# Both parts of every third weight unit made by GpSimd DMAs in a decoder layer with weights split in two

## The chip, the cores and the metric

The kernel runs on one core of a Trainium2 chip as a single program. A core has TensorE (matmuls; its weight loads are shown apart), VectorE, ScalarE, GpSimd and SyncE, each with its own queue of instructions that it works off in order, and 16 DMA engines that all queues share. The metric is the device time of one execution in microseconds, lower is better. The median of three runs before the change is 1499.94 us (1499.26 to 1501.11).

## The reference

One layer of a hybrid decoder on 256 tokens of width 2048, in float32. A normalised input goes through one large projection; its columns feed two mixers side by side (a gated DeltaNet with 8 heads and a block-sparse attention with 8 heads), both mixers are projected back, gated and added, and a gated feed-forward of inner width 5632 follows. Cut to what matters:

```python
u = _rmsnorm(h, norm_mix_w[l])
proj = jnp.einsum('btd,de->bte', u, w_in[l])
(q_a, k_a, v_a, z_a, beta_a, dec_a, q_b, k_b, v_b, gate_a, gate_b) = jnp.split(proj, split_at, axis=-1)
y_a = _gated_deltanet(q_a, k_a, v_a, z_a, beta_a, dec_a, conv_w[l], a_log[l], dt_bias[l], gdn_o_norm_w[l])
y_b = _moba_attention(q_b, k_b, v_b, q_norm_w[l], k_norm_w[l], rel_bias)
mix = (jax.nn.sigmoid(gate_a) * jnp.einsum('btc,cd->btd', y_a, w_branch_gdn[l])
       + jax.nn.sigmoid(gate_b) * jnp.einsum('btc,cd->btd', y_b, w_branch_moba[l]))
h = h + jnp.einsum('btd,de->bte', mix, w_out[l])
u = _rmsnorm(h, norm_ffn_w[l])
hid = jax.nn.silu(jnp.einsum('btd,df->btf', u, w_ffn_gate[l])) * jnp.einsum('btd,df->btf', u, w_ffn_up[l])
h = h + jnp.einsum('btf,fd->btd', hid, w_ffn_down[l])
```

## The kernel before

All weights lie in memory as one list of 504 units, in the order in which they are used. A unit is 128 partitions by 1024 float32, 512 KB. TensorE's format for the large products is fp32r, which is narrower than float32, so every operand is split into two: a high part, the value rounded to fp32r, and a low part, what the rounding left. A product is then three matmuls: high by high, low by high, high by low.

The class `Weights` (lines 39 to 73) makes the two parts of a unit. `load` (line 48) has SyncE issue a DMA of the unit into one of seven `wraw` buffers. `split` (line 56) has ScalarE copy it into a `whi` buffer with rounding (line 64) and VectorE subtract that from the raw unit into a `wlo` buffer (line 65); there are four buffers of each. `get(u)` loads up to unit u+5, splits up to unit u+2, and hands out unit u.

Two loops use units. `tm_job` (line 165) takes one unit for every two slices of the contraction: twelve matmuls of 512 columns, on lines 177 (high by high), 178 (low) and 179 (high by the activations' low part). In its order a unit's second matmul is the first that reads the low part, and its last one reads the high part. `fm_jobs` (line 143) is the same with the operands turned, for the 48 units of the DeltaNet's query, key and value. 456 units go through `tm_job`: the DeltaNet's output gate, the attention's projections, gates and branch projections, the output projection, 176 units of the feed-forward's first half (11 steps of sixteen units, each with one set of eight transposes, line 189), and 88 of the down projection.

Between the jobs, `tick` advances two chains of small steps for the mixers (DeltaNet from line 389, attention from line 629), which share ScalarE, VectorE and TensorE with the units and use GpSimd for some products of tiles. All of it lies in about the first 450 us. Six of the eight stores of the result are issued on GpSimd's queue, at the end (line 823).

The framework decides the order of instructions within an engine from dependencies and an estimate of its own, and puts in the waits; a buffer can be written again when the last instruction that reads it has ended.

Of the kernel before, what the change touches and what calls it, by code (L numbers as in the profile page):

```python
# [9 lines left out]
F32 = mybir.dt.float32  # L10
F32R = mybir.dt.float32r
I32 = mybir.dt.int32
AF = mybir.ActivationFunctionType
ALU = mybir.AluOpType
AX = mybir.AxisListType

P = 128
# [14 lines left out]
NPAR = 16 + 16 + 96 + 8 + 8 + 128 + 1 + 1  # L32

SPLIT_AHEAD = 3
RAW = 7
TICK = 8


class Weights:

    def __init__(self, nc, pool, src):
        self.nc, self.pool, self.src = nc, pool, src
        self.n = src.shape[0]
        self.raw, self.parts = {}, {}

    def load(self, u, cuts=1):
        if u in self.raw or u >= self.n:
            return  # L50
        t = self.raw[u] = self.pool.tile([P, 1024], F32, name="wraw", tag="wraw", bufs=RAW)
        for i in range(cuts):
            f = slice(i * 1024 // cuts, (i + 1) * 1024 // cuts)
            self.nc.sync.dma_start(t[:, f], self.src[u, :, f])

    def split(self, u):
        if u in self.parts or u >= self.n:
            return
        self.load(u)
        raw = self.raw[u]  # L60
        hi = self.pool.tile([P, 1024], F32R, name="whi", tag="whi", bufs=4)
        lo = self.pool.tile([P, 1024], F32R, name="wlo", tag="wlo", bufs=4)
        for f in (slice(0, 512), slice(512, 1024)) if u == 0 else (slice(0, 1024),):
            self.last_hi = self.nc.scalar.copy(hi[:, f], raw[:, f])  # L64
            self.last_lo = self.nc.vector.tensor_sub(lo[:, f], raw[:, f], hi[:, f].bitcast(F32))  # L65
        self.parts[u] = (hi, lo)

    def get(self, u):
        for k in range(u, u + RAW - 1):
            self.load(k)  # L70
        for k in range(u, u + SPLIT_AHEAD):
            self.split(k)
        return self.parts.pop(u)


# [1 line left out]
def layer(ctx: ExitStack, tc: tile.TileContext, xT, xtok, params, consts, relt, w_bd, w, out):  # L77
# [87 lines left out]
    def tm_job(act, nk):  # L165

        get = act if callable(act) else lambda kc: act[:, kc]
        ps = mm.tile([P, NT, 512], F32, name="ps", tag="mm")
        for kc in range(nk):
            if kc % 2 == 0:  # L170
                hi, lo = W.get(cursor[0])
                cursor[0] += 1
            sl = slice((kc % 2) * 512, (kc % 2) * 512 + 512)
            for n in range(NT):
                ah = get(kc)[:, n * P:(n + 1) * P]
                al = get(kc)[:, T + n * P:T + (n + 1) * P]
                nc.tensor.matmul(ps[:, n], ah, hi[:, sl], start=kc == 0, stop=False)  # L177
                nc.tensor.matmul(ps[:, n], ah, lo[:, sl], start=False, stop=False)  # L178
                nc.tensor.matmul(ps[:, n], al, hi[:, sl], start=False, stop=kc == nk - 1)  # L179
            if kc % (TICK // 2) == TICK // 2 - 1:  # L180
                tick()
        return ps
# [13 lines left out]
    with tc.tile_pool(name="xin", bufs=4) as xin:  # L196
# [4 lines left out]
        for c in range(1, KM // 4):  # L201
            nc.scalar.dma_start(xcs[c], xT[:, 4 * c:4 * c + 4])
        for u in range(1, RAW):
            W.load(u)
# [714 lines left out]
```

## Time and profile before

| | |
|---|---|
| median of three runs | 1499.94 us |
| the profiled execution, its own time | 1498.37 us |
| its span, first to last instruction | 1496.6 us |
| TensorE matmuls busy | 1474.1 us, 98% |
| VectorE busy | 868.9 us, 58% |
| ScalarE busy | 675.8 us, 45% |
| GpSimd busy | 56.7 us, 4% |
| memory read | 274.36 MB |
| DMA share of the span, SyncE's queue | 59.7% |
| granted TensorE clock | 1.000 |

A row of the costliest groups gives line, engine, operation, what is written from what, the shape, a count, then the busy time and the mean of one, and the idle time of the engine just before such instructions with what ended it. Matmuls overlap in the profile: one is shown as some 390 ns while one follows the other after less, so pace is read from the times of instructions and not from their durations. Issuing a DMA is not counted as busy; a DMA has a time from issue to landing.

### The profile page before, as it was taken

Reading aid. Unit: us, or ns where it says so; the run is one execution under the profiler, and the core shown is the slowest. Engines: PE = TensorE matmul, PEld = TensorE weight load, DVE = VectorE, ACT = ScalarE, POOL = GpSimd, SP = SyncE. Lnnn points to the kernel's source line nnn. Section 1 sums busy time; section 2 is a strip of 40 time slices with the busy share of each in tenths; the row PEclk is TensorE's granted clock in tenths of the full one; section 3 lists DMA queues with packets and bytes.
Section 4 is the critical chain, followed back from the end, with each engine's and each line's share of the span. In section 5 each row is a group of like instructions: output and inputs, shape, how many; then the busy total and the mean of one; then the engine's idle time right before and its main releaser. Section 6 shows DMA issues by size and latency. Waiting matters only on the chain.

```text
span 1496.6 us, 18724 instructions
## 1 busy us (share of the span) xinstructions
PE 1474.1 (98%) x7164; PEld 1227.0 (82%) x7164; DVE 868.9 (58%) x1161; ACT 675.8 (45%) x956; POOL 56.7 (4%) x48
## 2 busy tenths in 40 slices
PE   7999999999999999999999999999999999999998
PEld 6888778887878888888888888888888888888887
DVE  5978957866664445555565555555555555444443
ACT  6645445445454444444554444444444444333332
POOL 0003002301100000000000000000000000000000
PEclk9999999999999999999999999999999999999999
DMA  9564744753546666667666666666666566666661
GB/s 372 168 189 127 209 124 142 191 177 115 181 127 199 195 195 184 187 193 241 192 184 186 194 186 194 184 192 187 196 185 193 186 186 194 194 206 207 194 210 58
DMA packets 77450, 277.82 MB, mean 186 GB/s; under 512 B 8752, under 2 KB 9392, under 8 KB 76976
## 3 DMA queue, kind: packets, MB, share of 16 engines
q1 hardware_dynamic: 75456, 270.46, 59.7%
q10 hardware_dynamic: 1424, 4.59, 1.2%
q0 software_dynamic: 480, 1.57, 0.3%
q8 instruction: 56, 0.92, 0.3%
q14 instruction: 34, 0.28, 0.1%
HBM read 274.36 MB, written 2.23 MB: 185 GB/s over the span
## 4 chain that ended last, share of the span: by engine, by line
PE 91%; DVE 4%; DMA 2%; ACT 1%; issue 1%; POOL 0%; SPq 0%; DVEq 0%; ACTq 0%; POOLq 0%
PE ps L179 27%; PE ps L177 27%; PE ps L178 27%; PE ps L156 3%; PE ps L157 2%; PE pT L189 1%; DVE wlo L65 1%; DMA lb<-dm 1%; DMA bias<-in_relt 1%; DVE cacc L348 1%; DMA wraw<-in_w 0%; ACT whi L64 0%; PE pU L551 0%; PE pO L559 0%; PE pb L279 0%
## 5 line engine op out<-in xcount | busy, mean ns | idle before, releaser
L65 DVE TENSOR_TENSOR wlo<-wraw,whi 128x1024 fp32r<-128x1024 f32 (+1 forms) x505 | 619.9, 1229 | 521.7 <-ACT whi L64 519.7
L64 ACT CAST whi<-wraw 128x1024 fp32r<-128x1024 f32 (+1 forms) x505 | 530.0, 1051 | 680.2 <-PE ps L179 608.0
L177 PE MATMUL ps<-whi,uT 128*128 128x512 f32 x704 | 274.8, 390 | 0.0
L179 PE MATMUL ps<-whi,uT 128*128 128x512 f32 x704 | 273.9, 389 | 0.0
L178 PE MATMUL ps<-wlo,uT 128*128 128x512 f32 x704 | 273.9, 389 | 0.0
L177 PE MATMUL ps<-whi,aT 128*128 128x512 f32 x512 | 202.8, 396 | 0.0
L179 PE MATMUL ps<-whi,aT 128*128 128x512 f32 x512 | 201.3, 393 | 0.0
L178 PE MATMUL ps<-wlo,aT 128*128 128x512 f32 x512 | 200.4, 391 | 0.0
L179 PEld LDWEIGHTS ps<-whi,uT 128*128 128x128 f32 x704 | 132.2, 188 | 27.5
L177 PEld LDWEIGHTS ps<-whi,uT 128*128 128x128 f32 x704 | 132.2, 188 | 27.0
L178 PEld LDWEIGHTS ps<-wlo,uT 128*128 128x128 f32 x704 | 132.2, 188 | 27.0
L156 PE MATMUL ps<-aT,whi 128*128 128x512 f32 x384 | 137.6, 401 | 10.3 <-DVE aT L216 10.2
L179 PEld LDWEIGHTS ps<-whi,aT 128*128 128x128 f32 x512 | 96.2, 188 | 19.7
L177 PE MATMUL ps<-whi,high 128*128 128x512 f32 x288 | 112.0, 389 | 0.0
L178 PE MATMUL ps<-wlo,high 128*128 128x512 f32 x288 | 112.0, 389 | 0.0
L179 PE MATMUL ps<-whi,high 128*128 128x512 f32 x288 | 112.0, 389 | 0.0
L157 PE MATMUL ps<-aT,wlo 128*128 128x256 f32 x384 | 108.6, 283 | 3.1 <-DVE wlo L65 3.1
L178 PEld LDWEIGHTS ps<-wlo,aT 128*128 128x128 f32 x512 | 96.3, 188 | 18.7
L177 PEld LDWEIGHTS ps<-whi,aT 128*128 128x128 f32 x512 | 96.3, 188 | 18.4
L156 PEld LDWEIGHTS ps<-aT,whi 128*128 128x128 f32 x384 | 73.0, 190 | 27.4 <-DVE aT L216 10.2
L157 PEld LDWEIGHTS ps<-aT,wlo 128*128 128x128 f32 x384 | 73.4, 191 | 4.1 <-DVE wlo L65 4.0
L178 PEld LDWEIGHTS ps<-wlo,high 128*128 128x128 f32 x288 | 54.1, 188 | 11.3
(327 smaller groups left out, 1394.3 us busy)
## 6 DMA issues: line engine op xcount, KB each, us to landing
wraw<-in_w SPq DMA_DIRECT2D x503, 512.0 KB, 4.0
xrow<-in_xtok SPq DMA_DIRECT2D x1, 2048.0 KB, 10.2
lb<-dm ACTq DMA_DIRECT2D x2, 1024.0 KB
xr<-in_xtok SPq DMA_DIRECT2D x8, 256.0 KB, 5.5
xc<-in_xT ACTq DMA_DIRECT2D x3, 512.0 KB, 8.1
out<-fo POOLq DMA_DIRECT2D x6, 256.0 KB, 4.4
bias<-in_relt SPq DMA_DIRECT2D x4, 256.0 KB, 4.1
xc<-in_xT ACTq DMA_DIRECT2D x2, 256.0 KB, 5.0
```

Source lines behind the costliest of these rows:

```text
L64: self.last_hi = self.nc.scalar.copy(hi[:, f], raw[:, f])
L65: self.last_lo = self.nc.vector.tensor_sub(lo[:, f], raw[:, f], hi[:, f].bitcast(F32))
L156: nc.tensor.matmul(ps[:, j], hi[:, sl], act[:, kc], start=kc == 0, stop=False)
L157: nc.tensor.matmul(ps[:, j, :T], lo[:, sl], act[:, kc, :T], start=False, stop=kc == nk - 1)
L177: nc.tensor.matmul(ps[:, n], ah, hi[:, sl], start=kc == 0, stop=False)
L178: nc.tensor.matmul(ps[:, n], ah, lo[:, sl], start=False, stop=False)
L179: nc.tensor.matmul(ps[:, n], al, hi[:, sl], start=False, stop=kc == nk - 1)
L189: nc.tensor.transpose(p[:, i], src[:, i * P:(i + 1) * P], ident)
L348: nc.vector.scalar_tensor_tensor(acc[:, j, d:], u[:, j, :T - d], w[:, 3 - d:4 - d], acc[:, j, d:], op0=ALU.mult, op1=ALU.add)
```

## The change

Units 8, 11, 14 and so on up to 503 get their parts in another way. GpSimd issues a DMA of the unit into an fp32r buffer `dhi`, which rounds on the way: the high part. ScalarE writes that, times -1, into a buffer `dlo`. GpSimd then issues a second DMA of the same unit from memory that adds to `dlo`: the low part. There are two buffers each of `dhi` and `dlo`. The other units are made as before, with five `wraw` buffers where there were seven, and three each of `whi` and `wlo` where there were four. For a unit of the new kind, `get` issues the first DMA five units ahead, and multiplication and second DMA four units ahead.

```diff
-RAW = 7
+RAW = 5
+DMA_FROM, DMA_EVERY = 8, 3
...
+    def by_dma(self, u):
+        return u >= DMA_FROM and u % DMA_EVERY == DMA_EVERY - 1
 
     def load(self, u, cuts=1):
         if u in self.raw or u >= self.n:
+            return
+        if self.by_dma(u):
+            if u not in self.rounded:
+                self.rounded[u] = self.pool.tile([P, 1024], F32R, name="dhi", tag="dhi", bufs=2)
+                self.nc.gpsimd.dma_start(self.rounded[u], self.src[u])
             return
...
         self.load(u)
+        if self.by_dma(u):
+            hi = self.rounded[u]
+            lo = self.pool.tile([P, 1024], F32R, name="dlo", tag="dlo", bufs=2)
+            self.nc.scalar.mul(lo, hi.bitcast(F32), -1.0)
+            self.nc.gpsimd.dma_start(lo, self.src[u], accum_op=ALU.add)
+            self.parts[u] = (hi, lo)
+            return
         raw = self.raw[u]
-        hi = self.pool.tile([P, 1024], F32R, name="whi", tag="whi", bufs=4)
-        lo = self.pool.tile([P, 1024], F32R, name="wlo", tag="wlo", bufs=4)
+        hi = self.pool.tile([P, 1024], F32R, name="whi", tag="whi", bufs=3)
+        lo = self.pool.tile([P, 1024], F32R, name="wlo", tag="wlo", bufs=3)
...
     def get(self, u):
-        for k in range(u, u + RAW - 1):
+        for k in range(u, u + 6):
             self.load(k)
-        for k in range(u, u + SPLIT_AHEAD):
-            self.split(k)
+        for k in range(u, u + 6):
+            if k < u + SPLIT_AHEAD or (self.by_dma(k) and k < u + 5):
+                self.split(k)
         return self.parts.pop(u)
```

GpSimd's queue around the DeltaNet's first group, before (the names are tiles of that chain: `dec` decays, `mt` and `ct` products for its triangular solve):

```order
L399 TENSOR_TENSOR dec<-dec,gc 128x512 x2
L430 TENSOR_TENSOR mt<-dec,bk_1232 128x512
L430 TENSOR_TENSOR dec<-dec,rk_1228 128x512
L430 TENSOR_TENSOR mt<-dec,bk_1232 128x512
L430 TENSOR_TENSOR dec<-dec,rk_1228 128x512
L488 TENSOR_TENSOR k_1140<-k_1140,kd_1703 128x512
L460 TENSOR_TENSOR ct<-mt,cst 128x512 x2
L593 TENSOR_TENSOR rhs<-vs,rhs 128x512
```

The same place now (line 59 is the casting load, line 74 the accumulating one; the other lines have moved down by 18):

```order
L59 DMA dhi<-in_w 128x1024
L417 TENSOR_TENSOR dec<-dec,gc 128x512 x2
L74 DMA dlo<-in_w 128x1024
L59 DMA dhi<-in_w 128x1024
L448 TENSOR_TENSOR mt<-dec,bk_1225 128x512
L506 TENSOR_TENSOR k_1130<-k_1130,kd_1691 128x512
L448 TENSOR_TENSOR dec<-dec,rk_1221 128x512
L74 DMA dlo<-in_w 128x1024
L448 TENSOR_TENSOR mt<-dec,bk_1225 128x512
L448 TENSOR_TENSOR dec<-dec,rk_1221 128x512
L59 DMA dhi<-in_w 128x1024
L478 TENSOR_TENSOR ct<-mt,cst 128x512
```

A queue that held only the chain's operations now has two DMAs for every third unit, one after the other in turn, and the chain's operations stand between them.

ScalarE's queue in the feed-forward, before (line 64 is the copy of a split, line 811 the activation of the feed-forward):

```order
L64 CAST whi_8234<-wraw_8178 128x1024
L64 CAST whi_8252<-wraw_8196 128x1024
L64 CAST whi_8277<-wraw_8214 128x1024
L811 ACTIVATE fg_8268<-ps_8109,r2h_6511 128x512
L64 CAST whi_8295<-wraw_8232 128x1024
L811 ACTIVATE fg_8271<-ps_8109,r2h_6511 128x512
```

A like place now (line 81 is the copy, line 73 the multiplication by -1):

```order
L81 CAST whi_7933<-wraw_7878 128x1024
L81 CAST whi_7954<-wraw_7899 128x1024
L73 ACTIVATE dlo_7937<-dhi_7917 128x1024
L81 CAST whi_7986<-wraw_7931 128x1024
L81 CAST whi_8010<-wraw_7952 128x1024
L73 ACTIVATE dlo_7990<-dhi_7970 128x1024
```

Every third instruction of ScalarE's splits is now the multiplication, which waits for a casting load, and two copies of other units stand behind each.

GpSimd's queue at the same place now:

```order
L74 DMA dlo_7884<-in_w 128x1024
L59 DMA dhi_7917<-in_w 128x1024
L74 DMA dlo_7937<-in_w 128x1024
L59 DMA dhi_7970<-in_w 128x1024
L74 DMA dlo_7990<-in_w 128x1024
```

The accumulating load of one unit stands ahead of the casting load of the next.

## Rows read from the trace of the kernel before

**Rows 1.** The page's busy times: engine, us, share of the span, instructions.

```profile
PE 1474.1 (98%) x7164; PEld 1227.0 (82%) x7164; DVE 868.9 (58%) x1161; ACT 675.8 (45%) x956; POOL 56.7 (4%) x48
```

**Rows 2.** Table by stretch: busy us of engines, granted clock, DMA share, GB/s.

```profile
50.00:150.00 100.00, 98.22 (x555) 85.17 (x554) 84.82 (x160) 52.24 (x100) 13.25 (x9) 1.00 0.52 156
150.00:250.00 100.00, 96.86 (x622) 80.20 (x621) 76.50 (x145) 46.87 (x80) 8.71 (x6) 1.00 0.57 164
250.00:350.00 100.00, 99.94 (x613) 82.16 (x612) 66.52 (x123) 48.38 (x114) 17.54 (x11) 1.00 0.58 165
350.00:450.00 100.00, 97.33 (x499) 80.89 (x497) 70.44 (x145) 53.40 (x125) 11.64 (x8) 1.00 0.48 147
450.00:700.00 250.00, 250.00 (x1121) 207.47 (x1121) 130.57 (x124) 108.71 (x117) 0.00 (x0) 1.00 0.66 199
700.00:1230.00 530.00, 530.00 (x2397) 440.23 (x2396) 286.01 (x304) 234.03 (x274) 0.00 (x0) 1.00 0.64 190
```

**Rows 3.** Instructions in order of time, feed-forward: start, duration, what, idle before.

```profile
896.51 1.05 ACT L64 CAST whi<-wraw 128x1024 fp32r<-128x1024 f32 x1 [1.67 <-PE ps L179]
899.23 1.05 ACT L64 CAST whi<-wraw 128x1024 fp32r<-128x1024 f32 x1 [1.67 <-PE ps L179]
900.32 1.22 DVE L65 TENSOR_TENSOR wlo<-wraw,whi 128x1024 fp32r<-128x1024 f32 x1 [1.27 <-ACT whi L64]
```

**Rows 4.** The chain that ended last, in order of time: start, us, what.

```profile
121.97 1.23 DVE wlo L65
123.84 1.23 DVE wlo L65
...
128.01 4.00 DVE cacc L348 x5
...
147.14 14.65 DMA lb<-dm
...
857.50 0.87 PE pT L189 x8
901.92 0.87 PE pT L189 x8
```

**Rows 5.** The costliest groups: the two instructions of a split.

```profile
L65 DVE TENSOR_TENSOR wlo<-wraw,whi 128x1024 fp32r<-128x1024 f32 (+1 forms) x505 | 619.9, 1229 | 521.7 <-ACT whi L64 519.7
L64 ACT CAST whi<-wraw 128x1024 fp32r<-128x1024 f32 (+1 forms) x505 | 530.0, 1051 | 680.2 <-PE ps L179 608.0
```

**Rows 6.** GpSimd's output DMAs: issue in ns (min/median/max); KB and us to landing.

```profile
L823 POOL DMA_DIRECT2D out<-fo x6: 539/540/710, 1314.0 to 1433.8; - x6
...
out<-fo POOLq DMA_DIRECT2D x6, 256.0 KB, 4.4
```

**Rows 7.** Raw loads, KB and us to landing: 900 to 1000 us, then 0 to 60.

```profile
wraw<-in_w SPq DMA_DIRECT2D x36, 512.0 KB, 3.6
...
GB/s 0 149 254 333 389 418 415 423 410 397 380 404 421 399 412 418 404 453 459 393 352 401 410 418 393 328 257 19 25 257 262 287 232 3 246 104 0 0 0 0
...
wraw<-in_w SPq DMA_DIRECT2D x22, 512.0 KB, 7.3
```

**Rows 8.** GpSimd's operations by line: count, busy us, mean ns, idle before.

```profile
L460 POOL TENSOR_TENSOR ct<-mt,cst 128x512 f32<-128x512 f32 x4 | 8.7, 2187 | 0.0
L399 POOL TENSOR_TENSOR dec<-dec,gc 128x512 f32<-128x512 f32 x4 | 6.0, 1510 | 91.8 <-DVE dec L398 91.8
L593 POOL TENSOR_TENSOR rhs<-vs,rhs 128x512 f32<-128x512 f32 x2 | 3.4, 1717 | 134.4 <-DVE rhs L592 134.4
L604 POOL TENSOR_TENSOR o<-o,rq 128x512 f32<-128x512 f32 x2 | 2.1, 1042 | 14.4 <-DVE o L603 8.6 <-DVE rb1x L117 5.8
```

**Rows 9.** Table by stretch, the mixers' part as one row.

```profile
50.00:450.00 400.00, 392.35 (x2282) 328.42 (x2280) 298.28 (x571) 200.88 (x418) 51.14 (x34) 1.00 0.54 158
```

More of the change, by code (lines that the diff above doesn't have):

```diff
@@ L45, in __init__ @@
         self.n = src.shape[0]
-        self.raw, self.parts = {}, {}
+        self.raw, self.parts, self.rounded = {}, {}, {}
+    def by_dma(self, u):
+        return u >= DMA_FROM and u % DMA_EVERY == DMA_EVERY - 1
     def load(self, u, cuts=1):
         if u in self.raw or u >= self.n:
+            return
[3 more added lines that the diff above has]
+                self.nc.gpsimd.dma_start(self.rounded[u], self.src[u])
             return
```

## The prediction

> **What bounds the kernel now.** I read the busy shares first. TensorE is busy for 1474.1 of 1496.6 us; VectorE, the next, for 868.9 [rows 1]. An average hides stages, so the second view is the table by stretch. From 450 to 1230 us TensorE is busy for every microsecond, while VectorE and ScalarE are at about half; before 450 us it idles a little: 400 us less 98.22, 96.86, 99.94 and 97.33 is 7.65 us [rows 2]. The granted clock is 1.00, the 2.4 GHz level, in all of them. So splitting weights on ScalarE and VectorE is hidden work, except around 100 to 225 us, where VectorE is at 85% and then 77%. What relief of VectorE and ScalarE can give is at most those 7.65 us.
>
> The third view is the pace. ScalarE's splits in the feed-forward follow each other by 2.72 us, each released by TensorE [rows 3]: that is a unit of twelve matmuls. The transposes of two neighbouring sub-stages begin at 857.50 and 901.92 [rows 4], so sixteen units with one set of transposes take 44.42 us, 2.78 us a unit. All the rest is a question of how far ahead of TensorE a unit's parts are ready.
>
> **The change, part by part.** Units 8, 11, ... 503 are taken, 166 of 504. For each, ScalarE's copy (1051 ns) becomes a multiplication by -1 of the same size, which I cost the same, and VectorE's subtraction (1229 ns) goes [rows 5]: 166 x 1.229 = 204 us off VectorE, of which only the 7.65 us can show. I take 5 us, since some of the idle time is waiting for loads.
>
> Added are 332 DMAs on GpSimd's queue. GpSimd's busy total is 56.7 us [rows 1]; its six output DMAs took 540 ns each (710 at most) [rows 6], so 332 of them are 179 us: the engine itself has room.
>
> What matters is the loop that the two buffers of each kind close. The buffer of unit u is that of unit u-6, so its casting load cannot start before TensorE has left u-6; then the load lands, ScalarE multiplies, the accumulating load starts and lands, and only then does TensorE's second matmul of unit u have its weights. From the end of u-6 to the start of u there are five units: 5 x 2.78 = 13.9 us where there are transposes and 5 x 2.72 = 13.6 without, say 13.8. If the loop takes longer, TensorE waits for the difference once in six units (the two buffers' loops run beside each other, each with its own six units), and there are (504 - 8) / 6 = 82.7 such periods: **83 us per microsecond of excess.** Nothing is queued up to absorb it, since the next load starts only when TensorE has left the buffer.
>
> The loop's terms, none of which the trace shows directly:
> - Casting load, 512 KB. Between SP's plain load of the same bytes in the feed-forward, 3.6 us, and the same load with the queue full in the first 60 us, 7.3 us [rows 7]. Nearest is GpSimd's own DMA, the output: 256 KB in 4.4 us [rows 6]. The other 256 KB at the rate of a fully busy DMA (190 GB/s at a share of 0.64 in [rows 2], so 297 GB/s) are 0.9 us more: 5.3 us.
> - Multiplication, 1.05 us, and 0.2 us for the copy that may be running on ScalarE when it gets ready (44% busy, half a copy left).
> - Accumulating load. No row shows one. It cannot be quicker than the plain load, 3.6 us; the slowest row of its size is the broadcast reload of 1024 KB, 14.65 us [rows 4]. I assume that it handles the bytes twice, source and the tile that it adds to: 4.4 + 3 x 0.9 = 7.1 us, nearer to the lower rows because the reload is a broadcast out of memory just written.
> - Four hand-overs, 0.05 us each (VectorE starts at 900.32 after a copy that ended at 900.28 [rows 3]): 0.2 us.
>
> That is 5.3 + 1.25 + 7.1 + 0.2 = 13.85 us, just the 13.8 there are. But both loads also share the DMAs with the raw loads. Per three units now five times 524 KB are handled (two raw, one cast, two for the accumulation) in 8.3 us, 315 GB/s, over the 297 at which the present packets would fill the DMAs, though under the 380 to 459 that a full queue reached at the start [rows 7]. I stretch the two loads by 315/297, 6% of 12.4 us: 0.75 us. The loop is then 14.6 us, the excess 0.8 us: 65 us.
>
> The Trainium skill ("Collectives: The Full Stack", section on SDMA and CCE and "Why ReduceScatter is half of AllGather") says that an add in the DMA costs nothing by itself but needs two source reads, which halves the rate; my doubling agrees with it, and no run here shows it. The skill's "DMA: Bandwidth & Descriptors" (section "Anatomy of one DMA — SWDGE (gpsimd) path") puts such a DMA at 2.0 us plus its bytes at 436 GB/s. By that, 256 KB would take 2.6 us where the row has 4.4, so the trace disagrees; as an estimate from that page the two loads would be about 3.2 and 4.4 us and the loop under 10, which is the first rival below.
>
> The raw side is not the limit: ScalarE is in order, and the multiplication of unit u stands ahead of the copy of unit u-1. It waits until 5.3 us into the loop, is done at 6.6, and copy and subtraction end at 8.9, while unit u-1 starts four units in, at 11. That cover is gone if the casting load takes over 7.5 us, and then the raw units are late too.
>
> In the first 450 us GpSimd also has 34 tensor operations of 1.0 to 2.2 us in the same queue [rows 8], and the order puts many of them between the two loads of a unit. Busy for 51.14 us in all [rows 9], they delay a load where the loop has nothing to spare, and a load that waits holds them: the one that waited longest (134.4 us in two places) waited for VectorE. If a third of the 51 us lands on the loop, that is 17 us; less 5 us of relief, 12 us. In the down projection the output DMAs wait for VectorE between two loads, but the second of these still waits for ScalarE then: nothing.
>
> Sum: the profiled execution is 1498.4 us (span 1496.6 and 1.8 around it), 1.5 under the median of the runs. 1498.4 + 65 + 12 = 1575.4, and with the 1.5 us to the median **1577 us**, slower by 5%.
>
> **Rivals.**
> - *The loop fits, and VectorE's relief shows.* If the two loads take under about 12 us together, TensorE never waits for them after 450 us. For it: SP's 3.6 us for the same bytes, which would make even a doubled accumulation some 6 us. Against: GpSimd's 4.4 us for half the bytes. The time is 1498.4 less 3 to 7.65 us, 1491 to 1495. A third of this case is lost again to the tensor operations in GpSimd's queue and ends within 3 us of before.
> - *The loop fits, but GpSimd's queue does not.* Then only the first 450 us pay, 8 to 30 us: 1506 to 1528. For it: the chain there runs through VectorE's splits and taps [rows 4], so what comes late is not hidden. Against: nearly all of its 7.65 us of idle TensorE lie there too, and are refilled first.
> - *The accumulation is the bound.* At the 14.65 us of the reload the loop is 21.4 us, and the excess 7.6 us: 1498 + 630 = 2130 us. For it only that no row shows the operation.
> - *VectorE locks GpSimd out while it writes descriptors.* Each load would start up to one subtraction (1.23 us) late, 2.5 us a loop, 204 us more than I say: about 1780. Against: the six output DMAs have 539, 540 and 710 ns as least, median and most, beside a VectorE that is half busy [rows 6]. The rule is in the skill's "SBUF — State Buffer" (section "SBUF: two separate sides"): it holds for VectorE in a two-port mode. The trace shows no such lock.
>
> **How the numbers follow.** Loop over its room: 0.52. Accumulation far slower: 0.07, lock-out: 0.03. GpSimd's queue alone: 0.08. Loop fits and gains over 0.2% (3 us, about what a measurement of this kernel can tell): 0.21. Within 0.2%: 0.09. So faster 0.21, same 0.09, slower 0.70. The likeliest case's own range is an excess of 0.2 to 3 us, 1510 to 1750. The whole range starts at the best that relief can do, 1491, and ends at 1750.
>
> **What would show it.** Right: TensorE's waits for the accumulating load lead the table of waits from 450 us on, once in three or six units and about a microsecond long; the periods between transposes grow from 44.4 us to about 46.5; the DMA share is above 0.85; the accumulating load lands 6 to 9 us after its issue and the casting one after 5 to 6. Wrong: periods of 44.4 us as before, TensorE busy throughout from 450 us, and the landings together under 12 us; or, the other way, raw units that wait on ScalarE.

## The result and the profile after

The changed kernel takes **1702.72 us** (median of 4 runs, 1700.02 to 1711.97) against 1499.91 (4 runs, 1499.26 to 1501.11): a ratio of 1.1365 with a 95% interval of 1.135 to 1.138. It is slower by 203 us, where 77 were predicted: the sign was right, the size was not.

From the page after: busy times, GpSimd's and SyncE's DMA queues (packets, MB, share of 16 engines' span), the three kinds of load (KB each, median us from issue to landing):

```profile
PE 1534.7 (90%) x7164; PEld 1235.9 (73%) x7164; DVE 676.3 (40%) x995; ACT 657.3 (39%) x956; POOL 284.4 (17%) x380
...
q0 software_dynamic: 48288, 175.66, 46.6%
q1 hardware_dynamic: 51552, 183.42, 28.7%
...
wraw<-in_w SPq DMA_DIRECT2D x337, 512.0 KB, 6.0
dhi<-in_w POOLq DMA_DIRECT2D x166, 512.0 KB, 7.3
dlo<-in_w POOLq DMA_DIRECT2D x166, 512.0 KB, 5.5
```

VectorE lost 193 of its 868.9 us [rows 1], as the edit says, and no engine became the bound in its place: GpSimd, the only one whose share rose, is at 17%. The table by stretch shows that TensorE now idles everywhere, in the feed-forward too, where it was busy for every microsecond [rows 2]:

```profile
50.00:150.00 100.00, 92.46 (x488) 78.17 (x486) 63.02 (x132) 45.40 (x94) 21.83 (x26) 0.97 0.72 190
150.00:250.00 100.00, 83.74 (x555) 69.56 (x556) 63.07 (x118) 41.95 (x70) 14.17 (x17) 0.93 0.73 182
250.00:350.00 100.00, 85.01 (x398) 70.68 (x397) 57.40 (x119) 39.52 (x105) 32.22 (x34) 0.91 0.67 174
350.00:450.00 100.00, 92.97 (x553) 75.36 (x552) 45.11 (x88) 40.25 (x92) 21.89 (x24) 0.97 0.65 174
450.00:700.00 250.00, 227.75 (x1037) 183.62 (x1035) 94.42 (x137) 98.96 (x137) 35.19 (x50) 0.99 0.77 215
700.00:1230.00 530.00, 491.55 (x2140) 390.22 (x2139) 188.70 (x224) 204.71 (x255) 80.49 (x114) 0.99 0.80 227
```

The table of waits (who waited for what: us in total, times, longest) names a ring. GpSimd waits for ScalarE's multiplication, ScalarE for the casting load, TensorE for the accumulating load; GpSimd seldom for a buffer that TensorE must leave (15 times of 166 in the row of line 59, and 5 more behind line 175; from 700 to 1380 us once):

```profile
POOL dlo L74 <- ACT dlo L73: 1204.8, 154, 19.5
...
ACT dlo L73 <- DMA dhi<-in_w: 726.2, 154, 10.1
...
PE ps L196 <- DMA dlo<-in_w: 104.2, 100, 8.6
POOL dhi L59 <- PE ps L197: 68.8, 15, 11.8
```

Three units in order of time show the ring turning (start, us, what, idle before). First GpSimd, then ScalarE's multiplications:

```profile
1007.68 0.86 POOL L74 DMA_DIRECT2D dlo<-in_w  x1 [8.07 <-ACT dlo L73]
1008.22 0.87 POOL L59 DMA_DIRECT2D dhi<-in_w  x1
1017.18 0.85 POOL L74 DMA_DIRECT2D dlo<-in_w  x1 [8.09 <-ACT dlo L73]
1017.72 0.87 POOL L59 DMA_DIRECT2D dhi<-in_w  x1
...
1006.32 1.06 ACT L73 ACTIVATE dlo<-dhi 128x1024 fp32r<-128x1024 f32 x1 [4.71 <-DMA dhi<-in_w]
...
1015.83 1.06 ACT L73 ACTIVATE dlo<-dhi 128x1024 fp32r<-128x1024 f32 x1 [5.12 <-DMA dhi<-in_w]
```

The accumulating load of one unit is issued at 1007.68; 0.54 us later, right behind it, the casting load of the next such unit; that has landed 7.61 us later, when ScalarE starts (1015.83); 1.35 us after that start the next accumulating load goes out (1017.18). One turn of the ring is 0.54 + 7.61 + 1.35 = **9.50 us for three units**, where TensorE needs 44.41 x 3 / 16 = 8.33 [rows 4]. In this turn the DMA engines stand still between 1007.6 and 1009.2 us: no packet starts. The times from one set of transposes to the next, called periods below, agree:

```profile
923.53 0.60 PE L207 MATMUL pT<-ident,fg 128*128 128x128 f32 x4
...
972.93 0.60 PE L207 MATMUL pT<-ident,fg 128*128 128x128 f32 x4
```

Sixteen units take 49.40 us here, and 48.4 to 55.4 in the eleven periods of this kind, 50.0 on average: 9.38 us for three units, 1.05 more than TensorE needs.

Where the 201.5 us between the spans lie: the first transposes after the mixers begin at 660.8 us (577.3 before), 83.5 later; from there to the last ones 82.9 more are lost over 81 of the new units (1.02 us each); behind them 35.0.

### The profile page after: what moved, and what is told of

It is laid out like the page before. It is cut to its first block, busy times and chain, and to the rows that moved or that the text cites. A ratio compares the mean times of both kernels' runs of the same rounds, so it can differ in the third digit from the quotient of the medians.

```text
span 1698.1 us, 18720 instructions
## 1 busy us (share of the span) xinstructions
PE 1534.7 (90%) x7164; PEld 1235.9 (73%) x7164; DVE 676.3 (40%) x995; ACT 657.3 (39%) x956; POOL 284.4 (17%) x380
## 3 DMA queue, kind: packets, MB, share of 16 engines
q0 software_dynamic: 48288, 175.66, 46.6%
## 4 chain that ended last, share of the span: by engine, by line
issue 67%; POOL 12%; DMA 9%; PE 7%; DVE 2%; ACT 2%; POOLq 0%; DVEq 0%; ACTq 0%
POOL dhi L59 6%; DMA dhi<-in_w 6%; POOL dlo L74 4%; PE ps L196 2%; PE ps L197 2%; PE ps L195 1%; DMA wraw<-in_w 1%; DMA dlo<-in_w 1%; DVE wlo L82 1%; ACT whi L81 1%; ACT dlo L73 0%; PE ps L174 0%; POOL o L587 0%; POOL ct L478 0%; ACT junk L430 0%
## 5 line engine op out<-in xcount | busy, mean ns | idle before, releaser
L82 DVE TENSOR_TENSOR wlo<-wraw,whi 128x1024 fp32r<-128x1024 f32 (+1 forms) x339 | 420.0, 1244 | 857.0 <-ACT whi L81 856.5
L73 ACT ACTIVATE dlo<-dhi 128x1024 fp32r<-128x1024 f32 x166 | 176.1, 1061 | 728.6 <-DMA dhi<-in_w 726.2
L81 ACT CAST whi<-wraw 128x1024 fp32r<-128x1024 f32 (+1 forms) x339 | 350.8, 1041 | 171.0 <-PE ps L197 138.0
L74 POOL DMA_DIRECT2D dlo<-in_w x166 | 142.1, 856 | 1268.3 <-ACT dlo L73 1204.8
L195 PE MATMUL ps<-whi,uT 128*128 128x512 f32 x472 | 184.6, 391 | 0.0
L197 PE MATMUL ps<-whi,uT 128*128 128x512 f32 x472 | 183.8, 389 | 0.0
L59 POOL DMA_DIRECT2D dhi<-in_w x166 | 133.3, 803 | 89.9 <-PE ps L197 68.8
L196 PE MATMUL ps<-dlo,uT 128*128 128x512 f32 x232 | 97.6, 421 | 41.0 <-DMA dlo<-in_w 40.9
L195 PE MATMUL ps<-whi,aT 128*128 128x512 f32 x332 | 132.4, 399 | 0.0
L197 PE MATMUL ps<-whi,aT 128*128 128x512 f32 x332 | 131.0, 395 | 0.0
L195 PE MATMUL ps<-dhi,uT 128*128 128x512 f32 x232 | 91.8, 396 | 0.0
L197 PE MATMUL ps<-dhi,uT 128*128 128x512 f32 x232 | 91.8, 396 | 0.0
L195 PE MATMUL ps<-whi,high 128*128 128x512 f32 x192 | 75.2, 392 | 0.0
```

What stands on the lines that cost most here:

```text
L59: self.nc.gpsimd.dma_start(self.rounded[u], self.src[u])
L73: self.nc.scalar.mul(lo, hi.bitcast(F32), -1.0)
L74: self.nc.gpsimd.dma_start(lo, self.src[u], accum_op=ALU.add)
```

## The experiments

Theory Q: all of GpSimd's DMAs go through one queue, in order. An accumulating load, the casting load behind it, and the multiplication that needs the latter form one serial loop, one turn for three units. Theory L, that of the prediction: the loop of six units that two buffers close. Theory C: the DMAs have no capacity left.

**1 and 2. A third casting buffer, order kept or free.** Both have three `dhi` buffers (and four `wraw` for the space, so the loads of two constants move ahead by one raw load at the start); in the first the casting load of unit u+3 is held behind the accumulating load of u, as in the changed kernel.

```diff
-RAW = 5
+RAW = 4
-    ... name="dhi", tag="dhi", bufs=2)
+    ... name="dhi", tag="dhi", bufs=3)
 (first run only; that it notes last_acc is left out here)
+    with ExitStack() as after:
+        if self.last_acc is not None:
+            after.enter_context(self.tc.issue_after(self.last_acc.ins))
         self.nc.gpsimd.dma_start(self.rounded[u], self.src[u])
```

> A third dhi buffer (and four wraw buffers instead of five), with GpSimd's order held as in the change: the accumulating load of unit u stands ahead of the casting load of unit u+3. Theory Q (one serial loop through GpSimd's queue: accumulating load, casting load behind it, ScalarE's multiplication, next accumulating load, 9.3 us for three units): the buffer was not what was waited for, nothing changes, 1680 to 1720 us, the sixteen-unit periods of the feed-forward stay at 48 to 50 us. Theory L (the loop of the prediction, closed by the two buffers, five units of room): the casting load may start three units earlier, the wait goes, 1500 to 1530 us, periods of 44.4 us. Theory C (the DMAs can't carry the added traffic): as Q, within 2% of 1700 us.

> The same third dhi buffer and four wraw buffers, but the order left to the framework, which now puts the casting load of unit u+3 ahead of the accumulating load of unit u. Theory Q: the serial loop is open, feed-forward periods back to 44.4 to 45 us, only the first 450 us still pay: 1510 to 1550 us. Theory L: 1500 to 1530 us as well, but the run before must then have come down too. Theory C: the bytes are the same, so 1650 us or more.

Measured: 1658.25 us (one run) with the order kept; 1512.62 with the order free (4 runs; 1.0086, interval 1.0069 to 1.0103). GpSimd's queue with the order kept, then with it free:

```profile
999.70 0.87 POOL L77 DMA_DIRECT2D dlo<-in_w  x1 [7.86 <-ACT dlo L76]
1000.25 0.87 POOL L62 DMA_DIRECT2D dhi<-in_w  x1
1009.07 0.87 POOL L77 DMA_DIRECT2D dlo<-in_w  x1 [7.95 <-ACT dlo L76]
```

```profile
1005.87 0.55 POOL L59 DMA_DIRECT2D dhi<-in_w  x1 [6.41 <-PE ps L197]
1006.74 0.87 POOL L74 DMA_DIRECT2D dlo<-in_w  x1 [0.33 <-ACT dlo L73]
1014.92 0.55 POOL L59 DMA_DIRECT2D dhi<-in_w  x1 [7.31 <-PE ps L197]
```

The free order's feed-forward, and its landings:

```profile
700.00:1230.00 530.00, 530.00 (x2393) 440.00 (x2392) 211.38 (x241) 235.39 (x277) 89.76 (x126) 1.00 0.95 255
```

```profile
dhi<-in_w POOLq DMA_DIRECT2D x166, 512.0 KB, 6.1
dlo<-in_w POOLq DMA_DIRECT2D x166, 512.0 KB, 7.8
```

With the order kept, a turn takes 9.37 us in these rows and 9.2 on average over eleven periods of 49.0 us, third buffer or not (9.4 in the changed kernel). With it free, the multiplication finds its high part landed long before, GpSimd waits for TensorE again, and TensorE is busy for 530 of 530 us. The two loads together take longer there (13.9 us) than in the changed kernel (12.8): what counts is not their length but that one turn contained both a queueing behind the other load and the multiplication. L falls with the first run, in which a third buffer takes back only 44 of 203 us; C with the second: a DMA share of 0.95 costs the feed-forward nothing. Theory Q's own time for the first run, 1680 us or more, was missed as well. Of the 42 us between the two profiled spans, 32 come back before the first transposes (629.2 us, in the changed kernel 660.8), so there the buffer counts for something; in the feed-forward the periods are 45.2 to 52.8 us. Why some turns are shorter is open.

**3. The accumulating load alone.** Raw units by SyncE for all, ScalarE copies and multiplies.

```diff
-            if u not in self.rounded:
-                self.rounded[u] = ... "dhi" ...; self.nc.gpsimd.dma_start(self.rounded[u], self.src[u])
-            return
...
-            hi = self.rounded[u]
+            hi = self.pool.tile([P, 1024], F32R, name="dhi", tag="dhi", bufs=2)
+            self.nc.scalar.copy(hi, self.raw[u])
```

> The accumulating load alone: every third unit is loaded by SyncE like the others, ScalarE makes both dhi (copy) and its negative, GpSimd only issues the accumulating load. Same doubled accumulation, same bytes from memory. Theory Q: no casting load stands behind an accumulating one, so no serial loop: 1495 to 1530 us, feed-forward periods 44.4 us. Theory L: room for multiplication and accumulation (1.1 + 5.5 us) is there, 1495 to 1530 us. Theory C: the traffic is the same, 1600 us or more. Below 1497 us would be relief of VectorE showing in the first 450 us.

Measured: 1513.58 us (4 runs; 1.0091, 1.0072 to 1.011). All 166 accumulating loads are there, and the feed-forward has periods of 44.45 us. Without a casting load in the queue the loop is gone. An accumulating load lands after 7.2 us here, with raw loads around it.

**4. A plain load in place of the accumulating one.** The second load overwrites `dlo` instead of adding; it still rounds, as the first does.

```diff
-            self.nc.gpsimd.dma_start(lo, self.src[u], accum_op=ALU.add)
+            self.nc.gpsimd.dma_start(lo, self.src[u])
```

> The second load replaces dlo instead of adding to it (so the low part is the whole weight and the output is not the reference's); order, buffers and issue are those of the change. Its packets should fall from 328 ns to about 170 ns each, 3.4 us of data to about 1.7. Theory Q: the casting load queued behind it lands 1.7 us earlier, 5.6 us after issue, the serial loop is 7.6 us, under the 8.3 us of three units: feed-forward periods 44.4 us, 1510 to 1560 us in all. Theory L: 5.6 + 1.3 + 3.8 us, under 13.8 us: 1500 to 1530 us. Theory C: a fifth of the traffic gone, 1600 to 1650 us.

Measured: 1551.35 us (one run), feed-forward periods of 44.4 to 45.5 us. From its page:

```profile
dhi<-in_w POOLq DMA_DIRECT2D x166, 512.0 KB, 5.4
dlo<-in_w POOLq DMA_DIRECT2D x166, 512.0 KB, 4.4
```

The same order with a second load that is 1.1 us shorter, and a first one that therefore lands 1.9 us sooner: one turn is then 0.54 + 5.4 + 1.35 = 7.3 us, under 8.33. So the accumulation's length counts, but as a term of this loop. Of the 52 us that remain, 39 are lost before the first transposes; I have not taken them apart.

**5 and 6. Only the later, only the early units.** The new way from unit 152 on, and up to 151.

```diff
-DMA_FROM, DMA_EVERY = 8, 3
+DMA_FROM, DMA_EVERY = 152, 3
 (the other run)
-        return u >= DMA_FROM and u % DMA_EVERY == DMA_EVERY - 1
+        return DMA_FROM <= u < 152 and u % DMA_EVERY == DMA_EVERY - 1
```

> As the changed kernel, but only units from 152 on are made by GpSimd's DMAs (118 of them); the mixers' stage keeps the old way. Theory Q (the accumulating load, the casting load behind it in GpSimd's queue and the multiplication make one serial loop of about 9.3 us for three units that TensorE could do in 8.33) holds in the feed-forward by itself: the loop falls into that order without any help from the mixers, periods between transposes of 48 us or more, and 118 x 1.0 = about 118 us over before: 1600 to 1640 us. Rival D (GpSimd's tensor operations and the mixers' chain throw the loop out of step, and it would keep pace if it began undisturbed): periods of 44.4 us, 1498 to 1510 us.

> The other part alone: units 8 to 151 are made by GpSimd's DMAs (48 of them), from 152 on the old way. Theory Q: the loss is the sum over these units only, 48 x 1 to 1.5 us = 48 to 72 us, 1550 to 1575 us, and periods of 44.41 us in the feed-forward. With the run that has only the later units the two losses add up to the changed kernel's 203 us within some 20 us. Rival D: most of the loss would be here and be carried into the feed-forward, so the early units alone would cost nearly as little as they do without a standing delay, under 30 us, and the sum of the two would fall far short of 203 us.

Measured: 1637.98 and 1569.10 us (one run each), before 1499.39: +138.6 and +69.7, together 208.3, against the 203 of the whole change. Both runs also have the fewer buffers, whose 6.5 us (experiment 9 below) the sum counts twice. Spread over its units, the loss is 1.17 us for each of 118 later ones and 1.45 for each of 48 early ones. With only the early units the feed-forward runs at 44.41 us; with only the later ones, undisturbed by the mixers, at 50. Rival D falls. The start of the later units shows how the loop closes; GpSimd's queue, and then, in order, the landings of the first three of these loads:

```profile
533.21 0.60 POOL L59 DMA_DIRECT2D dhi<-in_w  x1 [139.09 <-PE ps L197]
539.93 0.87 POOL L74 DMA_DIRECT2D dlo<-in_w  x1 [6.12 <-ACT dlo L73]
541.36 0.55 POOL L59 DMA_DIRECT2D dhi<-in_w  x1 [0.56 <-PE ps L197]
551.54 0.87 POOL L74 DMA_DIRECT2D dlo<-in_w  x1 [9.62 <-ACT dlo L73]
552.09 0.88 POOL L59 DMA_DIRECT2D dhi<-in_w  x1
560.71 0.87 POOL L74 DMA_DIRECT2D dlo<-in_w  x1 [7.74 <-ACT dlo L73]
```

```profile
dhi<-in_w POOLq DMA_DIRECT2D x1, 512.0 KB, 5.0
...
dlo<-in_w POOLq DMA_DIRECT2D x1, 512.0 KB, 6.4
...
dhi<-in_w POOLq DMA_DIRECT2D x1, 512.0 KB, 8.7
```

The first casting load, with nothing ahead of it, lands in 5.0 us and its accumulating load goes out after 6.7. The second casting load comes 1.43 us behind that, when TensorE leaves its buffer, and needs 8.7 us, since the accumulating load (6.4) is ahead of it. So the second accumulating load is late by 551.54 - 539.93 - 8.33 = 3.3 us; by then the third casting load's buffer has long been free, and it is issued right behind. The next nine turns take 9.0 to 9.4 us. It takes one turn to fall into this, and nothing leads out of it, because nearly every turn is longer than the 8.33 us of TensorE's three units.

**7. Every fourth unit.**

```diff
-DMA_FROM, DMA_EVERY = 8, 3
+DMA_FROM, DMA_EVERY = 8, 4
```

> As the changed kernel, with every fourth unit instead of every third made by GpSimd's DMAs (124 instead of 166). Theory Q: the same serial loop of about 9.3 us now has four units, 11.1 us, to run in, so TensorE does not wait for it in the feed-forward: periods of 44.4 us, and only the first 450 us lose something, 1505 to 1540 us. Rival P (a price per unit made this way, 203 us / 166 = 1.22 us each, whatever the spacing): 124 x 1.22 = 151 us, about 1650 us, with periods of 44.4 + 4 x 1.22 = 49 us.

Measured: 1530.16 us (one run). 124 units instead of 166, and 31 us of loss instead of 203. The feed-forward's row:

```profile
700.00:1230.00 530.00, 530.00 (x2397) 440.09 (x2396) 229.06 (x260) 230.13 (x279) 67.96 (x96) 1.00 0.83 239
```

Four units give 11.1 us for a turn, and TensorE is busy throughout the feed-forward. There the new units have no price of their own; there is a threshold, one turn against the time of the units between. The 31 us are all lost before the first transposes (608.4 us, before 577.3); what loses them there is open.

**8, 9, 10 and 12. Versions meant to be faster, and the buffers alone.** 8: experiment 3 for sixteen units only. 9: no unit made by DMA, buffers as in the changed kernel. 10: as 8, with both parts by DMA and three casting buffers. 12: experiment 3 for twelve units, with the buffers of before.

```diff
 (8 and 10; 12 begins at 32)
+        return (20 <= u < 47 or 104 <= u < 125) and u % DMA_EVERY == DMA_EVERY - 1
 (9)
+DMA_FROM, DMA_EVERY = 1000, 3
 (12)
+RAW = 7
+            hi = self.pool.tile(..., name="dhi", tag="whi", bufs=4)
+            lo = self.pool.tile(..., name="dlo", tag="wlo", bufs=4)
```

> A version meant to be faster: the high part is again ScalarE's copy of a raw unit that SyncE loads, and only the low part comes from the accumulating load, for 9 units from 20 to 44 and 7 units from 104 to 122, where VectorE was busiest and TensorE idled before; none at the start, beside the two broadcast reloads or in the feed-forward. If relief of VectorE is worth what the earlier runs show in those places (2.4 us of TensorE's gaps between 125 and 150 us gone, 1.5 us between 400 and 425), and nothing else changes: 1494 to 1498 us. Rival: fewer raw and split buffers (five and three instead of seven and four) and the denser traffic cost as much as that, 1499 to 1504 us.

> No unit is made by GpSimd's DMAs; only the buffers are those of the changed kernel (five raw, three and three split buffers where there were seven, four and four). Theory Q charges the whole loss to the units made by DMA and nothing to the buffers: 1498 to 1502 us. Rival B (part of the loss of the fast variants, 7 us of the spot version and 13 us of the third buffer, is that fewer raw units are loaded and split ahead when VectorE runs late in the first 450 us): 1503 to 1508 us, with TensorE's waits for VectorE's splits between 75 and 225 us.

> The same sixteen units as in the spot version, with both parts made by GpSimd's DMAs, three casting buffers (four raw ones) and the order left free, as in the run with a third buffer. If the spot version's 7.6 us came from what precedes the accumulating load on ScalarE (copy and multiplication of a raw unit, 2.1 us for each of them), this ends at 1495 to 1500 us. If they come from the smaller number of raw and split buffers, it is no better, 1504 to 1512 us.

> A second version meant to be faster: the buffers of the kernel before (seven raw, four and four split), and for 5 units from 32 to 44 and 7 from 104 to 122 the low part by the accumulating load, written into the buffers of the ordinary low parts; the high part is ScalarE's copy. Theory: the run with the buffers alone has cost 6.4 us and the spot version 7.6, so the sixteen loads by themselves cost about 1 us, and the earliest units, whose delay made a new wait of 3.7 us at 82 us, are left out here; with the buffers back the time is 1495 to 1500 us. Rival: four low-part buffers, shared with a load that takes 7.2 us from issue to landing beside 2.1 us of copy and multiplication, are too few in three units' time (8.3 us), and the units behind come late: 1501 to 1510 us, with TensorE waiting for the accumulating load or the split behind it between 100 and 150 us.

Measured: 8: 1506.99 us (1.0049, 1.0035 to 1.0063); 9: **1506.34 us (1.005, 1.0038 to 1.0063)**; 10: 1515.11 (1.0108, 1.0093 to 1.0124); 12: 1509.30 (1.0068, 1.0054 to 1.0082); five runs each, four for 10. The buffers alone cost 6.5 us, to which theory Q had given nothing; nearly all of it is lost before the first transposes (periods of 44.45 us behind them). The mixers' stretch of 9, and TensorE's waits for a split in it:

```profile
50.00:450.00 400.00, 389.68 (x2251) 324.93 (x2250) 291.82 (x554) 197.44 (x408) 51.15 (x34) 1.00 0.53 157
```

```profile
PE ps L175 <- DVE wlo L82: 5.4, 4, 1.8
```

TensorE idles 2.7 us more there than in [rows 9], and its second matmul waits longer for VectorE's split (before the change 3.1 us in 3 times). Where the rest of the 6.5 us lies was not looked into. Between 8 and 9 the intervals overlap: sixteen accumulating loads gained nothing that can be measured. In 12 the rival's time came in, and its waits in part: TensorE waits for a split near 133 us and for a late accumulating load, though only near 365:

```profile
PE ps L192 <- DMA dlo<-in_w: 5.3, 1, 5.3
...
PE ps L171 <- DVE wlo L78: 2.8, 1, 2.8
```

The expectations of a faster kernel (8, 10 and 12) were all missed, and 8 and 10 end above their rivals' ranges too. In 10 TensorE has a gap of 4.5 us near 39 us; this run has four raw buffers instead of five, and three casting loads that go out in the first 3 us, and nothing here separates the two. No version beats the kernel before.

**11. The casting load alone.** SyncE loads the raw unit as well, VectorE subtracts.

```diff
-            return
...
-            self.nc.scalar.mul(lo, hi.bitcast(F32), -1.0)
-            self.nc.gpsimd.dma_start(lo, self.src[u], accum_op=ALU.add)
+            self.nc.vector.tensor_sub(lo, self.raw[u], hi.bitcast(F32))
```

> The casting load alone: for the same 166 units GpSimd's DMA makes the high part, SyncE loads the raw unit as well, and VectorE subtracts as before; no multiplication and no accumulating load. Theory Q: with nothing ahead of it in GpSimd's queue the casting load lands after about 5.4 us (5.4 beside a plain second load, 7.3 in the changed kernel), TensorE waits for no landing in the feed-forward, periods of 44.4 us, 1500 to 1515 us. Rival: the rounding itself makes it slow, 7 us or more as in the changed kernel.

Measured: 1540.31 us (one run). The landing is as expected, 5.7 us with no accumulating load in the queue, and the feed-forward has 44.4 to 44.7 us. The time is not: 1500 to 1515 were expected. 41 us are lost before the first transposes (618.6 us, before 577.3). Between 50 and 450 us TensorE waits for VectorE's ordinary splits, and VectorE's subtraction for a new unit waits for the casting load, with the rest of its work behind it in order. That the second wait causes the first is not shown:

```profile
dhi<-in_w POOLq DMA_DIRECT2D x166, 512.0 KB, 5.7
```

```profile
PE ps L194 <- DVE wlo L80: 9.3, 1, 9.3
PE ps L173 <- DVE wlo L80: 9.1, 3, 6.6
```

```profile
DVE dlo L72 <- DMA dhi<-in_w: 50.8, 16, 8.1
```

## Why the prediction was right or wrong

**The bound and the gain: right.** TensorE was the bound and relief of VectorE worth little. The 5 us that I took for it are not to be found in any run. **Not priced at all: the buffers** that the change takes from the old way, 6.5 us by experiment 9.

**The loop: this step failed.** "The two buffers' loops run beside each other, each with its own six units" is wrong. The loads of both loops stand in GpSimd's one queue, and the casting load of u+3 comes due while the accumulating load of u is on its way: by my own terms 8.3 us into u's loop, where the accumulating load goes out at 5.3 + 1.25 = 6.6 and takes 7.1. I checked each loop against its buffer and not the two against each other. What binds is a loop of three units and not of six: 9.4 us a turn against 8.33, a price of 1.05 us on 166 units in place of 0.8 us on 83. The later units alone lose 138.6 us (experiment 5, 6.5 of them the buffers), where 65 were predicted for the whole kernel (the prediction's own 0.8 us on 82.7 periods is 66).

What the loads wait for behind one another is seen in the landings: 5.0 us for a casting load with nothing ahead of it, 8.7 for the next, 1.43 us behind an accumulating one. The Trainium skill's "DMA: Bandwidth & Descriptors" states in its section "SWDGE vs HWDGE vs iDMA" that one queue only is allocated for the DMAs that GpSimd's software issues. The trace agrees: row q0 of the page after has 175.66 MB, all 332 new loads and the six outputs.

Its section "Queues, rings and completion order" adds that a DMA engine takes turns between queue rows, a whole packet at a time. One may expect from this that raw loads of SyncE get through while a second load of GpSimd has to wait. The trace does not show that: SyncE issued a raw load at 1009.60 us, and from 1009 to 1012 us 105 packets of GpSimd's queue start and none of SyncE's; that load lands after 6.3 us, where 3.6 was usual [rows 7]. The 38 raw loads that were issued 1 to 2 us behind an accumulating one (800 to 1380 us) take 6.3 us in the median. So the accumulating load holds up loads of another queue as well, and whether the casting load waits because of GpSimd's one queue, or because of the DMA engines that all queues share, is not shown. For the loop it is the same: what was issued first is in front.

**The sizes of the two loads: right for loads that do not queue behind each other.** The casting load was put at 5.3 us: 5.0 (alone), 5.4 (experiment 4), 5.7 (11). It is 7.3 in the changed kernel because it queues. The accumulating load was put at 7.1, stretched to about 7.5: 7.1 in experiment 8 and 7.2 in 3, with raw loads around it, and 7.8 in 2, behind a casting load; in the changed kernel 5.5, where the DMA engines often stand still when it goes out (1.3 us without a packet, in the median of 62 turns). Their sum, 13.1 with the stretch, is 12.8. The multiplication is 1.06 us.

**The DMAs' capacity: wrong in what it does.** I stretched the loads because the traffic (315 GB/s by my count) would pass what the packets can fill. Experiment 2 carries it at a share of 0.95 and loses nothing in the feed-forward; longer landings are hidden when the loads start early enough.

**GpSimd's tensor operations, 12 us: open.** The early units cost 69.7 us (experiment 6): 6.5 are the buffers, and 48 x 1.05 = 50 would be the loop if it cost there what it costs in the feed-forward. That would leave 13, but the 50 are not shown: experiments 4 and 7, whose turns fit, still lose 39 and 31 us before the first transposes. The clock has a part too. In the changed kernel the granted clock is 0.97, 0.93, 0.91 and 0.97 in the four rows from 50 to 450 us, where it was 1.00 [rows 2]: there are stretches at the 1.2 GHz level, and they follow TensorE's waits (in experiment 2 TensorE waits from 171.4 to 176.3 us, and the clock is at that level from 174.6 to 181.5). As an estimate from these rows, 3 + 7 + 9 + 3 = 22 us of work at 2.4 GHz are missing, if TensorE had work in all of them. Nothing here separates the loop, the clock and GpSimd's operations.

**The raw side: right.** TensorE's second matmuls of raw units waited 3.8 us in all for VectorE. The casting load's 7.3 us stay under the 7.5 at which I saw that cover go.

**The rivals.** That the accumulation alone is the bound falls with experiments 2 and 3. A lock by VectorE: a casting load's issue takes 534 ns on average in experiment 11 beside a VectorE that is half busy. An accumulating load's takes 0.86 us (median) in experiment 3, where nothing of GpSimd's DMAs is near it, and 0.53 when it only overwrites (experiment 4), so that is its own time; the casting loads of 0.87 us above are those right behind one. That the loop fits and gains would have needed the free order, and even that one (2) ends 13 us above before. The buffers cost 6.5 us in experiment 9, which has one raw buffer more; what else is lost lies in the first 500 us: at the start, where three casting loads go out beside the first raw ones (TensorE busy 34.88 us of 50, before 39.69), and around the two broadcast reloads (the first takes 20.12 us against 14.65 [rows 4]; granted clock 0.97 from 150 to 350 us).

**What would show it.** TensorE's waits for the accumulating load lead, as said. The periods are 50.0 and not 46.5 us, the DMA share is 0.80 and not over 0.85, and the two landings are the wrong way round, 5.5 and 7.3 where I said 6 to 9 and 5 to 6. That casting landing, longer than the accumulating one, is the sign of a casting load that stands behind the other.

## What to carry to other kernels

Before adding DMAs in pairs that depend on each other, write down for one turn every transfer that passes through the same queue, in order, and not only the buffers: a load that a computation waits for and that is queued behind another load pays for both. Such a loop has a threshold, so in the feed-forward spacing (every fourth unit), order (the first load of the next pair ahead of the second of this one) or a term shortened until the turn fits (experiment 4, 7.3 us against 8.33) took the loss away. Where the engine relieved is off the critical path there is little to win, and the buffers taken for it have a price of their own; run them alone first.

## What the runs showed of the hardware

- The accumulating load costs the DMA engines nearly twice a casting one, while it lands only 1.1 us later than the same load without the addition (5.5 us in the changed kernel against 4.4 in experiment 4). By the pages' queue rows (share x 16 x span / packets):

```profile
q0 software_dynamic: 24384, 88.62, 34.2%
```

```profile
q0 software_dynamic: 24384, 88.62, 18.3%
```

  The first is experiment 3 (span 1511.4 us): 339 ns a packet. The second is experiment 11 (span 1538.5): 185 ns. The ratio of 1.83 is near the factor of two that the prediction assumed.
- GpSimd issues a casting load in 0.53 us (experiment 11) and an accumulating one in 0.86 (experiment 3, 166 of them). A casting load right behind an accumulating one starts 0.54 us after it, before its 0.86 us are over, and then shows 0.87 us itself.
- In the changed kernel SyncE's raw loads hardly move while an accumulating load's packets run: between 800 and 1380 us, in 60 of 62 turns no packet of SyncE's queue starts during the middle four fifths of the accumulating load's packets. In experiment 3, where raw loads are more often under way already, 19% of the packets in such times are SyncE's.
- The core's 16 DMA engines ran at a share of 0.95 for 530 us (255 GB/s counted) without holding TensorE up once.
